# Three sums of weight blocks computed beside the convolution's projections, and the feed-forward's output gate started one chunk pair later

## The chip, the cores and the metric

The kernel runs on one core of a Trainium2 chip. A core has a matrix engine (PE, with its weight loads PEld), a vector engine (DVE), a scalar engine (ACT), GpSimd (POOL) and a queue engine (SP) that issues most transfers; 16 DMA engines move data between the chip's memory and the core. The metric is the device time of one launch in microseconds (us), lower is better. The kernel before took 958.01 us, the median of three runs (955.35 to 959.51).

## The reference, cut to what matters

One decoder block in float32, 512 tokens (S) of 1024 features (D): two mixers side by side, merged by sigmoid gates, then a SwiGLU feed-forward of 2816 hidden features. All matrix products are wanted to float32 accuracy.

```python
mod = silu(c) @ ada_w + ada_b                       # 6 vectors of 1024
sh_m, sc_m, gt_m, sh_f, sc_f, gt_f = split(mod, 6)
h = rmsnorm(x, norm_mix_g) * (1 + sc_m) + sh_m
q, k, v, g_ret, b_cv, c_cv, u_cv, g_a, g_b = split(h @ w_in, 9)
y_a = (silu(g_ret) * head_layernorm(retention(rope(q), rope(k), v))) @ ret_w_out
conv = causal_conv3(c_cv * u_cv, conv_w)
y_b = (b_cv * conv) @ conv_w_out
merged = sigmoid(g_a) * y_a + sigmoid(g_b) * y_b
x = x + gt_m * (merged @ mix_w_out)
h = rmsnorm(x, norm_ffn_g) * (1 + sc_f) + sh_f
f = (silu(h @ ffn_w_gate) * (h @ ffn_w_up)) @ ffn_w_down
x = x + gt_f * f
return rmsnorm(x, final_norm_g)
```

## The kernel before, in words

**Products.** Every float32 operand is split in a high part (ACT, a cast) and a low part (DVE, a subtraction), and a product is three matrix multiplications: high by low, low by high, high by high. A projection (`proj`) covers 256 output features: one weight load of 1 MB to a raw buffer, then for each half of 128 features a split and 24 matrix multiplications of 128 x 512. The raw buffers (tag `raw`) are three, and every large transfer uses one: a new load waits in SP's queue, in order, until the buffer it takes is given back. The split weights (tags `hi`, `lo`) have four buffers each, so that a split may run at most four halves ahead of PE.

**Stages in order of the program.** Values, keys, queries and gates of the retention, whose own steps are laid out between later projections by a counter (`after`, `tick`: each half of a projection is one tick); the convolution's projections for feature pairs p = 1 to 3, each c, u and b (in this text the convolution's loop); the loop over p = 0 to 3 with gate a, the retention's output product and 512 of the modulation's weights (`ada_load`, `mod_vecs`; the ga loop); the loop with gate b and the convolution's output product (the gb loop); the mix product in two halves of 512 columns, with the second norm between its token tiles; the feed-forward.

**Block sums.** The down product of the first 16 hidden chunks is done in two parts of eight chunks, each as a product of 2 x 2 blocks with seven multiplications in place of eight. It needs four sums of weight blocks per part. `block_sums` is a generator with eight steps, four per part: a step loads 1 MB of the down weights (two DMAs from SP) to a raw buffer, does four subtractions in place on DVE, and stores 1 MB to a scratch tensor from POOL's queue; its buffer is free when the store has landed. `next(block_steps)` does one step. Before, part 0's four steps stand at the end of the ga loop's four rounds, part 1's in the feed-forward.

**Output gates.** `gate_vec` computes gt_m or gt_f, spread over all partitions: for each of four pieces of 256 columns, at one tick a load of 1 MB (`ada_gt_m`, `ada_gt_f`), eight multiply-adds on DVE (`acc_gt_m`, `acc_gt_f`) and a split (`gh`, `gl`), and at the next tick a product with a matrix of ones on PE that spreads it (`gp_gt_m`, `gp_gt_f`). The gate gt_m is begun after the gb loop's first round; gt_f is begun after the first of part 0's four chunk pairs (q = 0).

**What sets the order.** In these stages the order on an engine is not the order of the text: the framework's scheduler places each instruction by its own account of when its inputs are ready, at compile time. On the chip each engine then runs its list in order. An instruction that waits holds everything behind it on its engine.

Of the kernel before, what the change touches and what calls it, by code (L numbers as in the profile page):

```python
# [70 lines left out]
def block_kernel(ctx, tc, x, c, positions, ada_w, ada_b, norm_mix_g, w_in, conv_w, ret_w_out,  # L71
# [18 lines left out]
    def scr(name, dt=F32, shape=None):  # L90
        return tp.tile(shape or [P, S], dt, tag="scr", bufs=12, name=name)

    def misc(name, dt=F32):
        return tp.tile([P, S], dt, tag="misc", bufs=6, name=name)

    def acc(name):
        return ps.tile([P, S], F32, tag="acc", bufs=4, name=name)
# [7 lines left out]
    def load_raw(src, k0, nk, n0, nn, name):  # L105
        t = wp.tile([P, nk, nn], F32, tag="raw", bufs=3, name=name)
        with tc.issue_after(load_raw.last.ins):
            load_raw.last = nc.sync.dma_start(
                t, src[k0 * P:(k0 + nk) * P, n0:n0 + nn].rearrange("(k p) n -> p k n", p=P))
        return t  # L110

    def split(view, shape, name, eng=None):
        hi = wp.tile(shape, F32R, tag="hi", name=name + "_h")
        act.copy(hi, view)
        lo = wp.tile(shape, F32R, tag="lo", name=name + "_l")
        (eng or vec).tensor_tensor(lo, view, hi.bitcast(F32), ALU.subtract)
        return hi, lo

    def split_act(src, name, hi=None, lo=None, eng=None):
        hi = slot(name + "_h", F32R) if hi is None else hi  # L120
        lo = slot(name + "_l", F32R) if lo is None else lo
        act.copy(hi, src)
        (eng or vec).tensor_tensor(lo, src, hi.bitcast(F32), ALU.subtract)
        return hi, lo
# [113 lines left out]
    def mod_vecs(f, j):  # L238

        pt = aux(f"mod_{f}{j}")  # L240
        a = ada_sum(ada_raw.pop((f, j)), 4 * P, f"{f}{j}")
        for i in range(4):
            mm(pt[:, i:i + 1], lhsT=a[:, i * P:(i + 1) * P], rhs=ones32[:, 0:1],
               start=True, stop=True)
        mod_cols(f, j, pt)
# [309 lines left out]
    def tick():  # L555
        due = [e for e in later if e[0] <= 1]
        later[:] = [[n - 1, fn] for n, fn in later if n > 1]
        for _, fn in due:
            fn()
# [4 lines left out]
    def conv_taps(p, i, pt, u, cv):  # L564
        vec.tensor_tensor(u, pt, u, ALU.mult)
        f = 2 * p + i
        cw = [vecs[0][:, R_CW + 8 * t + f:R_CW + 8 * t + f + 1] for t in range(3)]
        vec.tensor_scalar_mul(cv, u, cw[2])
        vec.scalar_tensor_tensor(cv[:, 1:S], u[:, 0:S - 1], cw[1], cv[:, 1:S], ALU.mult, ALU.add)
        vec.scalar_tensor_tensor(cv[:, 2:S], u[:, 0:S - 2], cw[0], cv[:, 2:S], ALU.mult, ALU.add)  # L570
# [66 lines left out]
    def fm_gemm(pt, wh, wl, Ah, Al, ts=slice(0, S)):  # L637
        for k in range(KT):
            xh, xl = (Ah[:, k, ts], Al[:, k, ts]) if Al is not None else Ah[k]
            kh, kl = (wh[k], wl[k]) if isinstance(wh, list) else (wh[:, k, :], wl[:, k, :])  # L640
            mm3(pt[:, ts], kh, kl, xh, xl, k == 0, k == KT - 1)
        return pt

    def proj(src, col, Ah, Al, name, eng=None):
        raw = load_raw(src, 0, KT, col, 2 * P, "w_" + name)
        for i in range(2):
            wh, wl = split(raw[:, :, i * P:(i + 1) * P], [P, KT, P], f"w_{name}{i}", eng)
            yield i, fm_gemm(acc(f"p_{name}{i}"), wh, wl, Ah, Al)
            tick()
# [101 lines left out]
    def block_sums():  # L751
        for part, (f0, nf) in enumerate(PARTS[:2]):
            for k in range(nf // 2):
                w = wp.tile([P, 2, D], F32, tag="raw", bufs=3, name=f"w_bl{part}{k}")
                for i in range(2):
                    r0 = (f0 + k + i * nf // 2) * P
                    with tc.issue_after(load_raw.last.ins):
                        load_raw.last = nc.sync.dma_start(w[:, i], ffn_w_down[0, r0:r0 + P, :])
                (b11, b12), (b21, b22) = ([w[:, i, j * S:(j + 1) * S] for j in range(2)]
                                          for i in range(2))  # L760
                vec.tensor_tensor(b11, b12, b11, ALU.subtract)
                vec.tensor_tensor(b12, b22, b12, ALU.subtract)
                vec.tensor_tensor(b22, b22, b11, ALU.subtract)
                vec.tensor_tensor(b21, b21, b22, ALU.subtract)
                nc.gpsimd.dma_start(blocks[part][:, k], w)
                yield

    block_steps = block_sums()
# [4 lines left out]
    for p in range(1, KT // 2):  # L773
        cc, uu = {}, {}
        for i, pt in proj(wi, COL["c"] + 2 * p * P, Hh, Hl, f"c{p}"):
            cc[i] = scr(f"c{p}{i}")
            act.copy(cc[i], pt)
        for i, pt in proj(wi, COL["u"] + 2 * p * P, Hh, Hl, f"u{p}"):
            uu[i] = scr(f"cv{2 * p + i}")
            conv_taps(p, i, pt, cc[i], uu[i])  # L780
        for i, pt in proj(wi, COL["b"] + 2 * p * P, Hh, Hl, f"b{p}"):
            vec.tensor_tensor(uu[i], pt, uu[i], ALU.mult)
            conv_in[2 * p + i] = split_act(uu[i], f"ci{2 * p + i}")


    def ret_out(p):
        raw = wp.tile([P, KT, 2 * P], F32, tag="raw", bufs=3, name=f"w_ya{p}")
        src = ret_w_out[0, :, 2 * p * P:2 * (p + 1) * P].rearrange(
            "(q h e c) n -> h e c q n", h=2, e=2, c=64)
        dst = raw.rearrange("p (q e) n -> p e q n", e=2)  # L790
        for h in range(2):
            for e in range(2):
                load_raw.last = nc.sync.dma_start(dst[64 * h:64 * h + 64, e], src[h, e])
        for i in range(2):
            wh, wl = split(raw[:, :, i * P:(i + 1) * P], [P, KT, P], f"w_ya{p}{i}")
            yield i, fm_gemm(acc(f"p_ya{p}{i}"), wh, wl, ret_in, None)
            tick()
# [5 lines left out]
    for p in range(KT // 2):  # L803
        sg = {}
        for i, pt in proj(wi, COL["ga"] + 2 * p * P, Hh, Hl, f"ga{p}"):
            sg[i] = scr(f"sga{p}{i}")
            act.activation(sg[i], pt, AF.Sigmoid)
        for i, pt in ret_out(p):
            vec.tensor_tensor(sg[i], pt, sg[i], ALU.mult)
            m_a[2 * p + i] = sg[i]  # L810
        ada_load("f", 2 * p)
        mod_vecs("f", 2 * p)
        next(block_steps)
    gate = {}

    def gate_vec(name):
# [238 lines left out]
    def block_acts(part, nf):  # L1055

        first, acts = [], {n: [] for n in ("a11", "a12", "a22", "s1", "s2", "s3", "s4")}
        tok = slice(0, HS), slice(HS, S)
        f0 = PARTS[part][0]
        for q in range(nf // 2):  # L1060
            for g in swiglu((f0 + 2 * q) * P):
                if len(first) < nf // 2:
                    k = len(first)
                    t = misc(f"a11_{part}{k}", F32R)
                    acts["a11"].append(split_act(g[:, tok[0]], "", t[:, tok[0]], t[:, tok[1]]))
                    first.append(g)
                    continue
                k = len(acts["s1"])
                a11, a21 = (first[k][:, i] for i in tok)
                a12, a22 = (g[:, i] for i in tok)  # L1070
                sums = [scr(f"s{part}{k}_{i}") for i in range(2)]
                (s1, s2), (s3, s4) = ([s[:, i] for i in tok] for s in sums)
                both = [split_act(g, f"a2_{part}{k}")]
                vec.tensor_tensor(s1, a21, a22, ALU.add)
                vec.tensor_tensor(s2, s1, a11, ALU.subtract)
                vec.tensor_tensor(s3, a11, a21, ALU.subtract)
                vec.tensor_tensor(s4, a12, s2, ALU.subtract)
                both += [split_act(s, f"s{part}{k}{i}") for i, s in enumerate(sums)]
                for i, n in enumerate(("a12", "a22", "s1", "s2", "s3", "s4")):
                    acts[n].append([z[:, tok[i % 2]] for z in both[i // 2]])  # L1080
            if part == 0 and q == 0:
                gate_vec("gt_f")
            if part == (0 if q == 3 else 1):
                next(block_steps)
        return acts
# [60 lines left out]
    for part in range(2):  # L1146
        block_down(part, block_acts(part, PARTS[part][1]))
# [78 lines left out]
```

## Time and profile before

| | before |
|---|---|
| median of three runs | 958.01 us (955.35 to 959.51) |
| the profiled execution | 957.96 us, span 956.2 us |
| granted PE clock, mean | 0.997 |
| PE busy | 940.0 us (98%) |
| DVE busy | 633.6 us (66%) |
| ACT busy | 362.1 us (38%) |
| DMA | 144.02 MB, mean 151 GB/s |

The span counts from the first to the last instruction; 1.76 us of the profiled execution lie around it. All helpers record their operations in lines 62 and 64 of the kernel, so that rows are told apart by their tiles: `w_gb_l<-w_gb,w_gb_h` is the low half of gate b's weights. A row gives its start and length in us, the engine, the operation, output and inputs, shape, count and, in brackets, the idle time before it and what ended that. PE's matrix multiplications overlap, so that the distance of their starts, not their length, is what one costs.

### The profile page before, as it was taken

The page shows a single profiled execution, that of the slowest core. Times are in us where ns is not written, and L with a number is a line of the kernel's source. Part 1 is how long each engine was busy: PE and PEld are TensorE (multiplying, and loading weights), DVE is VectorE, ACT ScalarE, POOL GpSimd, SP SyncE. Part 2 cuts the span into 40 slices and gives each one's busy share as a digit, 9 for nine tenths or more (in the row PEclk, how much of TensorE's full clock was granted, in tenths as well). Part 3 has the DMA queues.
Part 4 walks back from the last instruction along what each step waited for, and adds up shares of the span by engine and source line. Part 5 has one row for each costly group of instructions (what it writes and reads, how often), then busy time and mean ns, then how long its engine had stood idle before and what let it go on. Part 6 is the DMA issues. An engine that isn't in the chain of part 4 may idle for free.

```text
span 956.2 us, 11090 instructions
## 1 busy us (share of the span) xinstructions
PE 940.0 (98%) x4367; PEld 784.4 (82%) x4367; DVE 633.6 (66%) x981; ACT 362.1 (38%) x537; POOL 9.5 (1%) x26
## 2 busy tenths in 40 slices
PE   8999999999999999999998999999999999999997
PEld 8888888888888888888877887988888888888886
DVE  5989775899566855556367367766688536893356
ACT  7535333544444323222123234523443233532324
POOL 2000000000000000000000000000000000000000
PEclk9999999999999999999999999999999999999999
DMA  9943412332312257878556452454265752553202
GB/s 303 341 156 111 154 57 87 100 100 81 106 45 88 88 135 223 249 246 270 176 166 186 134 174 88 155 176 176 88 214 182 258 182 88 170 175 118 66 22 88
DMA packets 113619, 144.02 MB, mean 151 GB/s; under 512 B 4180, under 2 KB 93312, under 8 KB 112544
## 3 DMA queue, kind: packets, MB, share of 16 engines
q1 hardware_dynamic: 112048, 134.50, 44.3%
q0 software_dynamic: 1376, 8.57, 2.4%
q8 instruction: 34, 0.56, 0.3%
q10 hardware_dynamic: 144, 0.26, 0.1%
q14 instruction: 17, 0.14, 0.0%
HBM read 132.83 MB, written 10.49 MB: 150 GB/s over the span
## 4 chain that ended last, share of the span: by engine, by line
PE 81%; DMA 9%; DVE 7%; ACT 1%; issue 1%; SPq 1%; DVEq 0%; ACTq 0%
PE p_fu L64 12%; PE p_fg L64 12%; PE p_g L64 5%; PE p_v L64 5%; PE dn_t L64 5%; PE p_q L64 4%; PE p_k L64 4%; PE p_b L64 3%; PE p_u L64 3%; PE p_c L64 3%; PE dn_b L64 3%; DMA ada_gt_m<-in_ada_w_dram 3%; PE dn L64 3%; PE p_yb L64 2%; DMA blocks<-w_bl 2%; PE mix L64 2%
## 5 line engine op out<-in xcount | busy, mean ns | idle before, releaser
L64 PE MATMUL p_fg<-Gh,w_fg_l 128*128 128x512 f32 x160 | 62.3, 389 | 0.0
L64 PE MATMUL p_fg<-Gh,w_fg_h 128*128 128x512 f32 x160 | 62.3, 389 | 0.0
L64 PE MATMUL p_fu<-Gh,w_fu_l 128*128 128x512 f32 x160 | 62.3, 389 | 0.0
L64 PE MATMUL p_fg<-Gl,w_fg_h 128*128 128x512 f32 x160 | 62.2, 389 | 0.0
L64 PE MATMUL p_fu<-Gh,w_fu_h 128*128 128x512 f32 x160 | 62.2, 389 | 0.0
L64 PE MATMUL p_fu<-Gl,w_fu_h 128*128 128x512 f32 x160 | 62.2, 389 | 0.0
L64 DVE TENSOR_TENSOR w_fg_l<-w_fg,w_fg_h 128x1024 fp32r<-128x1024 f32 x20 | 24.4, 1222 | 33.1 <-ACT w_fg_h L64 33.1
L64 ACT CAST w_fu_h<-w_fu 128x1024 fp32r<-128x1024 f32 x20 | 21.1, 1053 | 63.7 <-PE p_fu L64 41.3
L64 ACT ACTIVATE fg<-p_fg 128x512 f32<-128x512 f32 x22 | 13.2, 598 | 76.0 <-PE p_fg L64 76.0
L64 DVE TENSOR_TENSOR w_b_l<-w_b,w_b_h 128x1024 fp32r<-128x1024 f32 x18 | 22.0, 1223 | 29.6 <-ACT w_b_h L64 29.6
L64 DVE TENSOR_TENSOR fg<-p_fu,fg 128x512 f32<-128x512 f32 x22 | 15.2, 691 | 38.6 <-PE p_fu L64 38.5
L64 PEld LDWEIGHTS p_fu<-Gl,w_fu_h 128*128 128x128 f32 x160 | 30.0, 188 | 6.2
L64 PEld LDWEIGHTS p_fg<-Gl,w_fg_h 128*128 128x128 f32 x160 | 30.0, 188 | 6.2
L64 PEld LDWEIGHTS p_fu<-Gh,w_fu_l 128*128 128x128 f32 x160 | 30.0, 188 | 6.2
L64 PEld LDWEIGHTS p_fg<-Gh,w_fg_h 128*128 128x128 f32 x160 | 30.0, 188 | 6.2
L64 PEld LDWEIGHTS p_fu<-Gh,w_fu_h 128*128 128x128 f32 x160 | 30.0, 188 | 6.2
L64 PEld LDWEIGHTS p_fg<-Gh,w_fg_l 128*128 128x128 f32 x160 | 30.0, 188 | 6.2
L64 DVE TENSOR_TENSOR sm<-st,dec 128x512 f32<-128x512 f32 (+3 forms) x32 | 15.6, 486 | 20.9 <-PE st L64 20.6
L64 DVE TENSOR_TENSOR w_bl<-w_bl 128x512 f32<-128x512 f32 x32 | 22.1, 689 | 8.0 <-DMA w_bl<-in_ffn_w_down_dram 7.4
L64 DVE TENSOR_TENSOR w_fu_l<-w_fu,w_fu_h 128x1024 fp32r<-128x1024 f32 x20 | 24.4, 1220 | 3.9 <-ACT w_fu_h L64 3.8
L64 PE MATMUL p_gb<-Hh,w_gb_l 128*128 128x512 f32 x64 | 25.2, 393 | 1.5 <-DVE w_gb_l L64 1.5
L64 ACT CAST sh<-sm 128x512 fp32r<-128x512 f32 (+3 forms) x32 | 14.7, 459 | 30.2 <-DVE sm L64 30.2
(420 smaller groups left out, 2732.5 us busy)
## 6 DMA issues: line engine op xcount, KB each, us to landing
w_fg<-in_ffn_w_gate_dram SPq DMA_DIRECT2D x11, 1024.0 KB, 5.6
w_fu<-in_ffn_w_up_dram SPq DMA_DIRECT2D x11, 1024.0 KB, 5.4
ada_m<-in_ada_w_dram SPq DMA_DIRECT2D x32, 256.0 KB, 5.8
ada_f<-in_ada_w_dram SPq DMA_DIRECT2D x32, 256.0 KB, 4.4
w_bl<-in_ffn_w_down_dram SPq DMA_DIRECT2D x16, 512.0 KB, 4.6
blocks<-w_bl POOLq DMA_DIRECT2D x8, 1024.0 KB, 6.1
w_t<-blocks SPq DMA_DIRECT2D x8, 1024.0 KB, 5.8
w_b<-in_ffn_w_down_dram SPq DMA_DIRECT2D x6, 1024.0 KB, 5.1
```

What stands on the lines that cost most here:

```text
L64: self.last = op(*args, **kw)
```

## The change

One block-sum step is put into each of the convolution's three rounds, between the c and the u projection. The ga loop keeps one step, in its first round. So the four steps of part 0 run earlier, and the ga loop's rounds 1 to 3 have none. The gate gt_f is begun after the second chunk pair (q = 1) instead of the first, so its eight ticks fall into pairs 2 and 3 instead of 1 and 2.

```diff
         for i, pt in proj(wi, COL["c"] + 2 * p * P, Hh, Hl, f"c{p}"):
             cc[i] = scr(f"c{p}{i}")
             act.copy(cc[i], pt)
+        next(block_steps)
         for i, pt in proj(wi, COL["u"] + 2 * p * P, Hh, Hl, f"u{p}"):
             uu[i] = scr(f"cv{2 * p + i}")
             conv_taps(p, i, pt, cc[i], uu[i])
...
         ada_load("f", 2 * p)
         mod_vecs("f", 2 * p)
-        next(block_steps)
+        if p == 0:
+            next(block_steps)
...
-            if part == 0 and q == 0:
+            if part == 0 and q == 1:
                 gate_vec("gt_f")
             if part == (0 if q == 3 else 1):
                 next(block_steps)
```

Three places show how the instructions move. The first is DVE in the convolution's first round, where the second of the moved sums (`w_bl_2740`) comes to stand among the retention's score products (`sm`), their splits (`sl`) and the splits of the b weights (`w_b_l`):

```order
L64 TENSOR_TENSOR sl_0_2302<-sm_0_2299,sh_0_2301 128x512
+L64 TENSOR_TENSOR w_bl_2740<-w_bl_2740 128x512
L64 TENSOR_TENSOR sm_7_2352<-st_7_2348,dec_2183 128x128
+L64 TENSOR_TENSOR w_bl_2740<-w_bl_2740 128x512
L64 TENSOR_TENSOR ci_l<-cv_722,ci_h 128x512
-L64 TENSOR_TENSOR w_b_l<-w_b_2553,w_b_h 128x1024
+L64 TENSOR_TENSOR w_b_l<-w_b_2561,w_b_h 128x1024
L64 TENSOR_TENSOR ci_l<-cv_727,ci_h 128x512
L64 TENSOR_TENSOR sl_7_2355<-sm_7_2352,sh_7_2354 128x128
L64 TENSOR_TENSOR sm_1_2365<-st_1_2361,dec_2293 128x384
+L64 TENSOR_TENSOR w_bl_2740<-w_bl_2740 128x512
L64 TENSOR_TENSOR sl_1_2368<-sm_1_2365,sh_1_2367 128x384
```

The score products `sm_7` and `sm_1` and their splits now have operations ahead of them that wait for the second sum's load. The second place is SP's queue from the ga loop's last round to the gate's first load; `w_ya` is the retention's output weight, `ada_f` the modulation's. Before:

```order
L108 DMA w_ga_3598<-in_w_in_dram 128x8x256
L793 DMA w_ya_3662<-in_ret_w_out_dram 64x4x256 x4
L64 DMA ada_f_0_3727<-in_ada_w_dram 128x2x256 x4
L64 DMA ada_f_4_3732<-in_ada_w_dram 128x2x256 x4
L758 DMA w_bl_3754<-in_ffn_w_down_dram 128x1024 x2
L108 DMA w_gb_3762<-in_w_in_dram 128x8x256
L108 DMA w_yb_3826<-in_conv_w_out_dram 128x8x256
L820 DMA gt_m_3898<-in_ada_b_dram 128x512
L820 DMA gt_m_3899<-in_ada_b_dram 128x512
L108 DMA w_gb_3902<-in_w_in_dram 128x8x256
L828 DMA ada_gt_m_3935<-in_ada_w_dram 128x8x256
```

And with the change:

```order
L108 DMA w_ga_3606<-in_w_in_dram 128x8x256
L794 DMA w_ya_3670<-in_ret_w_out_dram 64x4x256 x4
L64 DMA ada_f_0_3735<-in_ada_w_dram 128x2x256 x4
L64 DMA ada_f_4_3740<-in_ada_w_dram 128x2x256 x4
L108 DMA w_gb_3762<-in_w_in_dram 128x8x256
L108 DMA w_yb_3826<-in_conv_w_out_dram 128x8x256
L822 DMA gt_m_3898<-in_ada_b_dram 128x512
L822 DMA gt_m_3899<-in_ada_b_dram 128x512
L108 DMA w_gb_3902<-in_w_in_dram 128x8x256
L830 DMA ada_gt_m_3935<-in_ada_w_dram 128x8x256
```

The block sum's load is gone from between the modulation's and gate b's weights, and with it one user of a raw buffer; the order from there on is the same. The third place is DVE at the second norm of the first token tile, in the mix product's second half:

```order
L62 TENSOR_TENSOR n_0_r<-n2s_4404 128x1
-L64 TENSOR_SCALAR acc_gt_f_5071<-ada_gt_f_5069,cs 128x256
-L64 SCALAR_TENSOR_TENSOR acc_gt_f_5071<-ada_gt_f_5069,cs,acc_gt_f_5071 128x256 x3
L62 RECIPROCAL n_0_r<-n_0_r 128x1
-L64 SCALAR_TENSOR_TENSOR acc_gt_f_5071<-ada_gt_f_5069,cs,acc_gt_f_5071 128x256
L62 TENSOR_SCALAR xn_00_4623<-x_0_0_4386,n_0_r 128x512
L62 TENSOR_SCALAR xn_01_4625<-x_0_1_4387,n_0_r 128x512
-L64 SCALAR_TENSOR_TENSOR acc_gt_f_5071<-ada_gt_f_5069,cs,acc_gt_f_5071 128x256
L62 TENSOR_SCALAR h_00_4658<-tx_00_4648,a_f,s_f 128x128 x2
-L64 SCALAR_TENSOR_TENSOR acc_gt_f_5071<-ada_gt_f_5069,cs,acc_gt_f_5071 128x256 x2
```

The gate's sums no longer stand between the norm's statistics, its reciprocal and the scaled rows (`xn`); they come after the last `Gl` of the fourth token tile.

## The prediction

> **What bounds the kernel now.** I read first the page's busy table, then the table by stage (stage by stage the length, then busy time and count of PE, PEld, DVE, ACT and POOL, the granted clock, DMA share and GB/s), then PE's rows in order of time for every place where it sat idle.
>
> ```profile
> PE 940.0 (98%) x4367; PEld 784.4 (82%) x4367; DVE 633.6 (66%) x981; ACT 362.1 (38%) x537; POOL 9.5 (1%) x26
> ```
>
> ```profile
> 255.80:363.10 107.30, 107.30 (x491) 89.22 (x490) 73.14 (x100) 40.29 (x60) 0.00 (x0) 1.00 0.32 98
> 363.10:453.60 90.50, 90.50 (x417) 75.51 (x415) 51.60 (x74) 23.19 (x27) 2.15 (x4) 1.00 0.80 249
> 453.60:549.10 95.50, 90.91 (x394) 73.93 (x394) 49.98 (x81) 24.99 (x35) 0.00 (x0) 0.98 0.52 165
> ```
>
> The stages are the convolution's loop, the ga loop (gate a and the retention's output) and the gb loop (gate b and the convolution's output). PE sets the time. It never idles in the convolution and ga loops, though the four sums of weight blocks make DMA 80% busy in the latter. It idles in the gb loop (90.91 of 95.50), in the mix product and once after it. The rows where it does:
>
> ```profile
> 480.71 0.39 PE L64 MATMUL p_gb<-Hh,w_gb_h 128*128 128x512 f32 x1
> 482.57 0.50 PE L64 MATMUL p_gb<-Hh,w_gb_l 128*128 128x512 f32 x1 [1.47 <-DVE w_gb_l L64]
> ...
> 514.33 0.58 PE L64 MATMUL gp_gt_m<-gl_gt_m,onesr 128*128 128x256 f32 x1 [2.82 <-DVE gl_gt_m L64]
> ...
> 515.35 0.63 PE L64 MATMUL p_yb<-ci_l,w_yb_h 128*128 128x512 f32 x1
> 515.78 0.63 PE L64 MATMUL p_yb<-ci_h,w_yb_h 128*128 128x512 f32 x1
> ...
> 583.15 1.09 PE L62 MATMUL tx<-ident,xn 128*128 128x128 f32 x8 [1.92 <-DVE xn L62]
> ...
> 611.77 0.38 PE L64 MATMUL p_fg<-Gl,w_fg_4h 128*128 128x256 f32 x1 [0.58 <-DVE Gl L62]
> ```
>
> ```profile
> 527.24 0.24 PE gp_gt_m L64 x2
> 538.39 10.88 PE p_yb L64 x48
> ```
>
> The gb loop's work is eight such stretches of 10.88 and four spreads of 0.24, 88.0 us; it lasts 95.5. So 7.5 us are lost there, of them 2.82 and 1.47 in the two rows above, and some 1.3 by matmuls that after the long wait start 0.43 us apart (515.35, 515.78) where 48 normally take 10.88, 0.227 each.
>
> Why DVE is late there stands in the chain of waits:
>
> ```profile
> 445.73 8.83 DMA blocks<-w_bl
> ...
> 454.62 0.38 SPq L108
> ...
> 455.10 8.56 DMA ada_gt_m<-in_ada_w_dram
> ...
> 469.64 8.24 DMA ada_gt_m<-in_ada_w_dram
> ...
> 483.01 8.89 DMA ada_gt_m<-in_ada_w_dram
> ```
>
> ```profile
> 463.69 0.36 DVE L64 TENSOR_SCALAR acc_gt_m<-ada_gt_m,cs 128x256 f32<-128x256 f32 x1 [11.41 <-DMA ada_gt_m<-in_ada_w_dram]
> 481.30 1.22 DVE L64 TENSOR_TENSOR w_gb_l<-w_gb,w_gb_h 128x1024 fp32r<-128x1024 f32 x1
> ```
>
> Three raw buffers serve all weights. The ga loop's fourth block sum keeps one until its store lands (445.73 + 8.83 = 454.56). SP waits for that with the gb load at 454.62, and the first gate load stands behind it. The sums of the gate, and the weight splits queued behind them on DVE, then run one load after the other: 455.1, 469.6, 483.0.
>
> **The change, part by part.**
>
> *Three block sums leave the ga loop.* Per sum one 1 MB load in two DMAs, four DVE operations (692 ns in the row of the convolution part below, some 0.65 apart), one 1 MB store. The four instructions and two DMAs cost PE nothing where they leave, since PE was full there; the gain is the earlier start of the gb loop's chain. Without the store the gb load at 454.62 takes the buffer of the last retention-output weights, and the first gate load needs only the buffer of the gb weights before it. That one is free when its second split is done, and this split waits for PE to leave the last ga product:
>
> ```profile
> 441.96 0.39 PE L64 MATMUL p_ya<-ri_h,w_ya_l 128*128 128x512 f32 x1
> ```
>
> So 441.96, ACT's cast and DVE's 1.2: about 444.2 in place of 455.1. It lands near 453 (8.6 as in the chain), and its sum of eight operations at 0.5 (1.53 for three in the row at 580.65 below), with what DVE does between, ends near 457 in place of 468.5. From there each load follows the sum before it: 458 and 471 for 469.6 and 483.0, some 12 us earlier. The split that PE awaited at 482.57 is then done near 470, and the third spread's operand near 503, where PE without waits arrives at 508.6. Every wait of this loop has 5 us of cover and more, so I take nearly the whole: **-7.4**. Bounds: 0 (the chain is self-paced and stays) and 7.5.
>
> [...]
>
> *The feed-forward's gate starts one chunk pair later.* Its loads and sums stood inside the second norm, in DVE's queue:
>
> ```profile
> 573.82 6.41 DMA ada_gt_f<-in_ada_w_dram
> ```
>
> ```profile
> 578.77 0.16 DVE L62 TENSOR_TENSOR n_r<-n2s 128x1 f32<-128x1 f32 x1 [0.85 <-ACT n_j L62]
> 580.26 0.35 DVE L64 TENSOR_SCALAR acc_gt_f<-ada_gt_f,cs 128x256 f32<-128x256 f32 x1 [1.33 <-DMA ada_gt_f<-in_ada_w_dram]
> 580.65 1.53 DVE L64 SCALAR_TENSOR_TENSOR acc_gt_f<-ada_gt_f,cs,acc_gt_f 128x256 f32<-128x256 f32 x3
> 582.09 0.15 DVE L62 RECIPROCAL n_r<-n_r 128x1 f32<-128x1 f32 x1
> ...
> 609.72 0.35 DVE L64 TENSOR_SCALAR acc_gt_f<-ada_gt_f,cs 128x256 f32<-128x256 f32 x1 [1.50 <-DMA ada_gt_f<-in_ada_w_dram]
> ```
>
> The reciprocal needs only ACT's root (some 0.6 after 578.77, the norm's add, so 579.4); it ran at 582.09, and PE's transposes at 583.15 in place of about 581.1, where its matmuls before ended (583.15 less the wait). Without the four operations the norm is ready at 580.5: the wait of 1.92 goes, with its restart about 2.1. The Gl row that PE awaited at 611.77 stood behind three gate operations that began at 609.72; that wait of 0.58, 0.7 with restart, goes too. **-2.8**, bounds -2.0 and -2.9.
>
> Where do the gate's sums go? Into chunk pairs three and four, each load (5.6 to 7.6 us to landing) queued behind a split that frees its buffer.
>
> ```profile
> DMA to landing us min/median/max: 5.6/6.3/7.6
> ```
>
> ```profile
> 666.36 0.24 PE gp_gt_f L64 x2
> 666.60 10.91 PE p_fg L64 x48
> 677.51 10.88 PE p_fu L64 x48
> ```
>
> With each load at 7, sums of eight operations at 0.5 and the splits paced by PE, I get the four sums done at about 618, 633, 648 and 660. Their spreads stand in PE's queue at 652, 663, 674.3 (677.5 less 2.8, one 0.24 spread fewer ahead) and 685.4. The third is the tight one: its low half is queued on DVE behind the third pair's sums and splits and comes near 671, 3.5 us ahead of PE. Cost taken 0; with each of three loads 2 us later than I took, some 2.5. The next block sum's load moves from 646.5 to about 657; its product is not read before the second part of the feed-forward.
>
> *Three block sums enter the convolution's loop*, between the c and the u weights. PE is full there, so this can only cost. DVE is 68% busy; three sums add 12 x 0.65 = 7.8 us to 73.1 in 107.3, which fits on average. Two things are added: the DVE operations wait in order for their load, and each sum holds a raw buffer until its store lands (4.1 to 8.8 us). The first and third sum's rows fall into idle DVE time, or ahead of work with 2 us and more to spare. The second is the tight one:
>
> ```profile
> DMA to landing us min/median/max: 3.6/4.7/8.8
> ...
> L64 DVE TENSOR_TENSOR w_bl<-w_bl x32: 677/692/695, 362.7 to 760.4; 128x512 f32<-128x512 f32 x32
> ```
>
> ```profile
> 257.22 0.37 SPq L108 DMA_DIRECT2D w_u<-in_w_in_dram  x1
> ```
>
> ```profile
> 258.87 0.69 DVE L64 TENSOR_TENSOR sl<-sm,sh 128x512 fp32r<-128x512 f32 x1 [0.74 <-ACT sh L64]
> 261.72 0.29 DVE L64 TENSOR_TENSOR sm<-st,dec 128x128 f32<-128x128 f32 x1 [2.16 <-PE st L64]
> ...
> 266.66 0.56 DVE L64 TENSOR_TENSOR sl<-sm,sh 128x384 fp32r<-128x384 f32 x1 [0.63 <-ACT sh L64]
> ```
>
> ```profile
> 268.67 0.28 PE L64 MATMUL y<-sl,v_h 128*128 128x128 f32 x1
> 269.48 0.34 PE L64 MATMUL y<-sl,v_h 128*128 128x384 f32 x1
> ```
>
> Its load takes the buffer that at 257.22 went to the next u weights, behind the c load that waits for the first sum's store (done near 256). It lands at 257.65 + 4.7 = 262.4, between 261.3 and 266.4. DVE, idle from 259.5, stands at its first operation until then; behind it wait the score products and their splits (sm, sl) that PE reads at 268.67 and 269.48. After landing these need 4.1 and 5.7 us (two or three sums of 0.6, a split of 1.1, three of 0.6 and less). So PE waits only if the load lands after 263.8. Cost taken **+0.3**, bounds 0 and 2.6 (landing at 266.4), with a clock dip 3.9. The next u and b loads move from 257 and 272 to about 272 and 277; PE reads them at 308 and 320, so that is covered.
>
> **Sum.** The profiled execution took 957.96 us (span 956.2 and 1.76 around it), as good as the median of 958.01. 957.96 - 7.4 - 2.8 + 0.3 = **948.1**.
>
> **Rivals.**
>
> *The gb loop stays as it is.* DVE's order there is unchanged, and its period of load and sum, 14.5 and 13.4 us between the gate loads, is longer than the 10.9 that PE leaves. If it paced itself from the start, only the 2.8 would be won: 955.2. Against it: the second load waited for sums that began at 463.69 only because the first was issued at 455.1.
>
> *Part given back.* The second block sum's load lands late (2.6, clock dip 1.3) or the third spread comes late (2.5): 951 to 954. For it: DVE at both places waits in order for a load.
>
> *VectorE and the raw buffers become the bound in the convolution's loop.* Slower than before. Each sum then costs its full 2.6 on DVE and 2.8 of landing wait (259.5 to 262.4): 3 x 5.4 = 16.2 less 10.2 is +6, **964**. It decides when the three sums together cost PE more than 10.2, so when DVE has no idle time left before the score products. For it, ten-microsecond stretches where DVE is full:
>
> ```profile
> 290.00:300.00 10.00, 10.00 (x47) 8.04 (x46) 9.70 (x15) 5.24 (x10) 0.00 (x0) 1.00 0.33 105
> ```
>
> Against it: the order puts none of the new operations in such a stretch; it puts them where DVE in the trace is at 241, 247, 260 to 270 and 302 to 308 us, and the row at 261.72 shows it idle there for 2.16.
>
> **How the numbers follow.** Forecast 0.74, the loop that stays 0.09, part given back 0.09, slower 0.08; the strict reading of the clock rule, 949.4, is about a tenth of the forecast's share. Two kernels of this length can be told apart from about 0.5% on, 4.8 us, so faster means below 953.2. The forecast and most of the third case are faster: 0.80. Same: the second case and the rest, 0.12. Slower: 0.08. Range: the best of the bounds, 957.96 - 7.5 - 2.9 = 947.6, less 2.7 by which the runs before lie below their median, gives 945; above, the part given back and nearly the loop that stays: 955.
>
> **What would show it.** Right: PE without idle rows between 453 and 622, spreads of gt_m unwaited, no slow matmuls, the first gate load near 444, the ga loop's DMA share well below 0.80. The convolution's loop stays within 0.5 us of 107.3. Wrong: idle PE before a `y<-sl` row near 268 or before `gp_gt_f` near 674 (third case); acc_gt_m still waiting 5 us and more for loads with PE behind it (second); 110 us and more for the convolution's loop (slower).

## The result, and the profile after

The changed kernel takes 947.43 us (median of four runs, 947.26 to 948.23) and the kernel before 957.87 us beside it (955.35 to 959.51). The ratio is 0.9895, with a 95% interval of 0.9872 to 0.9917: faster by 1.05%. The prediction was 948.1 us in a range of 945 to 955. The profiled execution took 947.26 us, with a span of 945.2.

The first line of the page of after, the busy time of each engine:

```profile
PE 936.5 (99%) x4367; PEld 783.7 (83%) x4367; DVE 634.4 (67%) x981; ACT 363.2 (38%) x537; POOL 9.5 (1%) x26
```

The table by stage of after, in the columns of the prediction's table; the rows are the convolution's loop, the ga loop and the gb loop:

```profile
254.71:362.01 107.30, 107.30 (x492) 89.25 (x491) 77.75 (x108) 40.32 (x60) 1.07 (x2) 1.00 0.45 146
362.01:452.51 90.50, 90.50 (x417) 75.52 (x415) 47.35 (x68) 23.17 (x27) 0.53 (x1) 1.00 0.69 204
452.54:540.74 88.20, 88.20 (x395) 73.11 (x394) 47.83 (x75) 25.76 (x35) 0.00 (x0) 1.00 0.49 154
```

PE is busy in the whole of all three, at the full clock. The convolution's loop carries the three sums (DVE 77.75 in place of 73.14 us) and is not longer. The gb loop is shorter by 7.3 us. The places that the prediction spoke of, from the time-ordered rows of SyncE (SP), VectorE (DVE) and PE: first the loads of the gate gt_m,

```profile
443.87 0.59 SPq L830 DMA_DIRECT2D ada_gt_m<-in_ada_w_dram  x1
455.47 0.57 SPq L830 DMA_DIRECT2D ada_gt_m<-in_ada_w_dram  x1
468.95 0.55 SPq L830 DMA_DIRECT2D ada_gt_m<-in_ada_w_dram  x1
```

then VectorE at the second norm, and PE's transposes behind it,

```profile
570.41 0.16 DVE L62 TENSOR_TENSOR n_r<-n2s 128x1 f32<-128x1 f32 x1 [0.85 <-ACT n_j L62]
572.01 0.16 DVE L62 RECIPROCAL n_r<-n_r 128x1 f32<-128x1 f32 x1 [1.45 <-ACT n_r L62]
572.21 0.48 DVE L62 TENSOR_SCALAR xn<-x,n_r 128x512 f32<-128x512 f32 x1
```

```profile
572.75 1.09 PE L62 MATMUL tx<-ident,xn 128*128 128x128 f32 x8
```

The transposes have no bracket, so PE did not wait; the reciprocal comes 1.6 us after the norm's add, where it came 3.3 us after it before. With the first matrix multiplications of the stages as bounds (the mix product is counted to the start of its last one), the two profiled executions compare so (us):

| stage | before | after | difference |
|---|---|---|---|
| up to the convolution's loop | 255.78 | 254.70 | -1.08 |
| convolution's loop | 107.32 | 107.30 | -0.02 |
| ga loop | 90.55 | 90.55 | 0.00 |
| gb loop | 95.46 | 88.20 | -7.26 |
| mix product with the second norm | 48.14 | 46.11 | -2.03 |
| first chunk pair's projections | 24.90 | 24.00 | -0.90 |
| the rest | 334.04 | 334.32 | +0.28 |

Of the last two rows 0.24 is one spread of gt_f, which now stands in the rest. The two kernels are the same up to the convolution's loop, so that the 1.08 us there are not the change's; the 9.9 that are left are. In the other profiled kernels but one the convolution's loop begins at 254.73 to 255.29 us, so the profiled execution of the kernel before began it late.

### The profile page after: what moved, and what is told of

The parts are those of the page before. It is cut to its first block, busy times and chain, and to the rows that moved or that the text cites. A ratio compares the mean times of both kernels' runs of the same rounds, so it can differ in the third digit from the quotient of the medians.

```text
span 945.2 us, 11083 instructions
## 1 busy us (share of the span) xinstructions
PE 936.5 (99%) x4367; PEld 783.7 (83%) x4367; DVE 634.4 (67%) x981; ACT 363.2 (38%) x537; POOL 9.5 (1%) x26
## 3 DMA queue, kind: packets, MB, share of 16 engines
q1 hardware_dynamic: 112048, 134.50, 44.7%
## 4 chain that ended last, share of the span: by engine, by line
PE 98%; DVE 0%; ACT 0%; issue 0%; POOL 0%; ACTq 0%; POOLq 0%
PE p_fu L64 13%; PE p_fg L64 12%; PE p_ga L64 5%; PE p_g L64 5%; PE p_gb L64 5%; PE p_v L64 5%; PE p_yb L64 5%; PE dn_t L64 5%; PE p_ya L64 5%; PE p_q L64 5%; PE p_k L64 4%; PE p_b L64 3%; PE p_u L64 3%; PE p_c L64 3%; PE dn_b L64 3%; PE dn L64 3%
## 5 line engine op out<-in xcount | busy, mean ns | idle before, releaser
L64 ACT CAST w_fu_h<-w_fu 128x1024 fp32r<-128x1024 f32 x20 | 21.1, 1054 | 60.5 <-PE p_fu L64 34.2
L64 DVE SCALAR_TENSOR_TENSOR acc_f<-ada_f,cs,acc_f 128x512 f32<-128x512 f32 x28 | 21.0, 750 | 8.7 <-DMA ada_f<-in_ada_w_dram 7.8
L64 ACT CAST w_b_h<-w_b 128x1024 fp32r<-128x1024 f32 x18 | 18.9, 1051 | 18.6 <-PE p_fu L64 8.0
```

Of the source, the lines that this page charges most:

```text
L64: self.last = op(*args, **kw)
```

## The experiments

All of them are edits of the changed kernel. Times are medians, with the 95% interval of the ratio to the kernel before that ran beside them (its medians there lay between 956.3 and 958.1 us).

**One part alone: the sums.** The gate's start is put back:

```diff
-            if part == 0 and q == 1:
+            if part == 0 and q == 0:
                 gate_vec("gt_f")
```

> Only the three block sums move to the convolution's loop; the feed-forward's gate begins where it did before. Theory (the parts are independent): the gb loop takes 88.0 us instead of 95.5, the second norm keeps its two waits (about 1.9 us before the first transposes, 0.6 us before the first product with Gl), so about 950.2 us, 2.8 above the full change. Rival (the second norm's waits came from everything being late behind the gb loop): the waits go here too and the time is that of the full change, 947.4 us.

951.1 us (ratio 0.9897 to 0.9943). The gb loop takes 88.20 us, and the second norm keeps its waits, as the theory of independent parts has it. PE's rows there:

```profile
575.26 1.77 PE L62 MATMUL tx<-ident,xn 128*128 128x128 f32 x8 [2.04 <-DVE xn L62]
576.68 0.77 PE L62 MATMUL mix<-w_mix_h,mg_l 128*128 128x512 f32 x1
...
605.74 0.39 PE L64 MATMUL p_fg<-Gl,w_fg_4h 128*128 128x256 f32 x1 [0.80 <-DVE Gl L62]
```

The transposes and the multiplications behind them run slow here (1.77 us for eight, where the kernel before takes 1.09; the granted clock of the stage is 0.97), so the stage of the mix product takes 49.90 us, 1.8 more than in the kernel before, which waited 1.92 us at this place and kept its clock (1.00). That makes up the 1.7 us by which the profiled execution (951.93 us) lies above the expected 950.2; the median lies 0.9 above.

**The other part alone: the gate.** The four sums stay in the ga loop:

```diff
             act.copy(cc[i], pt)
-        next(block_steps)
...
-        if p == 0:
-            next(block_steps)
+        next(block_steps)
```

> Only the feed-forward's gate begins one chunk pair later; the four block sums stay in the ga loop. Theory: the second norm's two waits go and nothing else changes, about 955.1 us (2.8 below before), the gb loop still 95.5 us. Rival (the gate only pays where the loads before it are early): nothing is won, 957.9 us.

953.26 us (0.9926 to 0.9967), against 955.1 expected. The mix product takes 46.11 us and the first pair's projections 24.01, so the gate's part is worth 2.03 + 0.66 without the other. The gb loop takes 95.15 us, nearly the 95.46 of before. The profiled execution took 954.5 us and reached the convolution's loop 0.8 us sooner than that of the kernel before; with that, the expectation holds. That the median lies 1.2 us below the profiled execution is left open.

**Only the last of the three sums is moved.** The ga loop keeps a sum in rounds 0, 1 and 2, the fourth round has none, and the convolution's loop has one:

```diff
-        next(block_steps)
+        if p == 2:
+            next(block_steps)
...
-        if p == 0:
+        if p < 3:
             next(block_steps)
```

> One block sum in the convolution's loop (its third round), and the ga loop keeps three, in its first three rounds, with none in the fourth; the gate as in the full change. Theory (the fourth sum's hold of a raw buffer until its store lands is all that made the gate loads late): the first gate load is issued near 444 us and the gb loop takes 88.0 us, so 947.4 us, as the full change. Rival (the transfers of the sums crowd the ga loop's loads, a share for each sum): a third of the gain in the gb loop is there, its 95.5 us become 93.0, and the time is about 952.4 us.

947.63 us (0.9870 to 0.9907): the whole gain, and the gb loop at 88.20 us. The other two moves add nothing to it. What costs is a sum in the ga loop's last round.

```profile
445.35 0.59 SPq L831 DMA_DIRECT2D ada_gt_m<-in_ada_w_dram  x1
```

**The bytes without the buffer, first try.** A copy of 1 MB inside the device's memory in each of the ga loop's rounds 1 to 3, issued by GpSimd:

```diff
+        else:
+            nc.gpsimd.dma_start(spare[p], ffn_w_down[0, p * 2 * P:(p + 1) * 2 * P, :])
```

> The full change, and in the second to fourth round of the ga loop a copy of 1 MB within the device's memory that uses no buffer of the kernel: the bytes of the three sums are moved again where they were, with no raw buffer held and no work on VectorE. Theory (the buffer, not the bytes): the ga loop's DMA share rises again to about 0.8 and the time stays at 947.4 us within 0.5. Rival (the bytes): the loads of the gate come as late as before, the gb loop takes about 95.5 us and the time is about 954.9 us.

956.92 us (0.9979 to 1.0002), near the rival's number, but for another reason. The copies wait for nothing, and GpSimd's queue issued all three at the start of the program, between 5.6 and 8.3 us. The table by stretch of its first 60 us, this kernel:

```profile
0.00:20.00 20.00, 10.67 (x71) 10.28 (x72) 5.24 (x14) 10.87 (x25) 7.04 (x21) 0.91 0.88 316
20.00:60.00 40.00, 39.60 (x211) 34.25 (x211) 32.24 (x62) 19.80 (x35) 0.00 (x0) 0.96 1.06 338
```

and after:

```profile
0.00:20.00 20.00, 17.96 (x129) 17.43 (x130) 10.42 (x26) 14.65 (x33) 5.23 (x18) 1.00 0.94 304
```

PE is busy for 10.67 of the first 20 us in place of 17.96, and the convolution's loop begins at 264.06 us in place of 254.70. From there on nothing is lost (gb loop 88.20). So the run says nothing on the question; it prices 3 MB in the start-up, where the DMA share is 0.94 without them, at 9.4 us.

**The bytes without the buffer, in their place.** The same copies in SyncE's queue, where the sums' loads had stood:

```diff
+        else:
+            with tc.issue_after(load_raw.last.ins):
+                load_raw.last = nc.sync.dma_start(
+                    spare[p], ffn_w_down[0, p * 2 * P:(p + 1) * 2 * P, :])
```

> As traffic, but the three copies of 1 MB stand in SyncE's queue where the loads of the three sums stood in the kernel before, so that they run in the second to fourth round of the ga loop. Theory (the buffer, not the bytes): the ga loop's DMA share rises from 0.69 towards 0.8, the first gate load is still issued near 444 us, the gb loop takes 88.0 us and the time is 947.4 us within 0.5. Rival (the bytes): the gate's loads come late again, the gb loop takes some 95 us and the time is about 954.9 us.

947.34 us (0.9875 to 0.9908). The ga loop, and the first gate load behind it:

```profile
362.00:452.50 90.50, 90.50 (x417) 75.49 (x415) 44.98 (x64) 23.05 (x27) 0.53 (x1) 1.00 0.82 238
```

```profile
445.30 0.59 SPq L835 DMA_DIRECT2D ada_gt_m<-in_ada_w_dram  x1
```

The DMA share is 0.82, as high as before the change (0.80), the gate load comes as early as in after, and the gb loop takes 88.20 us. The bytes are not the cause.

**Six sums in the convolution's loop,** two in each round:

```diff
         next(block_steps)
+        next(block_steps)
...
-        if p == 0:
-            next(block_steps)
...
-            if part == (0 if q == 3 else 1):
+            if part == 1 and 1 <= q < 3:
                 next(block_steps)
```

> Two block sums in each of the three rounds of the convolution's loop, six in all, none in the ga loop, and the last two where they were; the gate as in the full change. Theory (the loop has room on VectorE, and only a load that lands late costs): VectorE is busy 85.6 of 107.3 us there, a second sum queued behind the first costs PE up to 1 us a round, the loop takes 107.3 to 110.3 us and the time is 947.4 to 950.4 us. Rival (VectorE and the raw buffers bound the loop from here on): each further sum costs its full 5.4 us of work and landing wait, the loop takes about 123 us and the time is about 963 us.

953.06 us (0.9935 to 0.9964), between the two: the loop takes 112.83 us, 5.5 more. Its row in the table by stretch, SyncE at the second round's loads, VectorE, and PE's wait:

```profile
255.17:368.00 112.83, 107.95 (x492) 89.09 (x491) 82.07 (x115) 40.20 (x60) 2.13 (x4) 1.00 0.59 191
```

```profile
257.48 15.55 SPq L758 DMA_DIRECT2D w_bl<-in_ffn_w_down_dram  x4
```

```profile
277.19 0.69 DVE L64 TENSOR_TENSOR w_bl<-w_bl 128x512 f32<-128x512 f32 x1 [5.36 <-DMA w_bl<-in_ffn_w_down_dram]
...
283.16 0.68 DVE L64 TENSOR_TENSOR sq_l<-sq,sq_h 128x512 fp32r<-128x512 f32 x1
```

```profile
283.90 0.50 PE L64 MATMUL var<-sq_l,blkr 128*128 128x512 f32 x1 [2.89 <-DVE sq_l L64]
```

VectorE is idle for 31 of the 113 us, so it is not full. It stands for 5.36 us at the second sum, whose load waited for a raw buffer, and the layer norm's `sq_l` behind it comes too late for PE. The same happens in the third round (1.76 us of PE's time). This is the mechanism that the prediction feared for the second sum; with one sum a round there is a free buffer, with two there is none.

**A held buffer without the sum.** At the end of the ga loop's last round a raw buffer is taken with a small load, touched by one VectorE operation of 128 x 8, and sent to memory and back in a chain of small transfers:

```diff
+        if p == 3:
+            w = wp.tile([P, 2, D], F32, tag="raw", bufs=3, name="w_hold")
+            with tc.issue_after(load_raw.last.ins):
+                load_raw.last = nc.sync.dma_start(w[:, 0, 0:8], ffn_w_down[0, 0:P, 0:8])
+            vec.tensor_tensor(w[:, 0, 0:8], w[:, 0, 0:8], w[:, 0, 0:8], ALU.add)
+            for i in range(3):
+                nc.gpsimd.dma_start(spare[i], w[:, 0, 0:8])
+                if i < 2:
+                    nc.gpsimd.dma_start(w[:, 0, 0:8], spare[i])
```

> The full change, and at the end of the ga loop's fourth round a raw buffer is taken and held, without the sum: 4 KB are loaded into it, VectorE adds 128x8 elements, and the buffer goes to the device's memory and back in five transfers of 4 KB, one after the other, at some 2 us each, so that it comes free near 455 us. Nearly no bytes and no work are added. Theory (the held buffer alone makes the gate's loads late): the gb load and the first gate load behind it are issued near 455 us, the gb loop takes 93 to 95.5 us and the time is 952 to 955 us; each us by which the buffer comes free earlier than 455 gives some of it back. Rival (the sum's work or its bytes, or the two together, made them late): the gb loop takes 88.2 us and the time is 947.4 us.

948.18 us (0.9885 to 0.9931), gb loop 88.20. The transfers were quicker than expected: the first gate load was issued at 449.23, which is still covered. Two kernels with longer chains (`range(4)` and `range(5)`, store and load each time) followed:

> As hold_only, with eight transfers of 4 KB in place of five (each took some 2 us there, and the buffer came free at 448.7 us), so that the raw buffer comes free near 454.6 us, as in the kernel before. Theory (the held buffer alone): the first gate load is issued near 455.1 us, the gb loop takes 93 to 95.5 us in place of 88.2 and the time is 952.5 to 955 us. Rival (a held buffer is covered; the sum's work on VectorE or its bytes are needed for the loss): 88.2 us, and 948 us.

> As hold_long with ten transfers, so that the buffer comes free some 4 us later, near 458.6 us. Theory: PE already waits for every further us of delay there, so the gb loop is about 4 us longer than in hold_long and the time is 956 to 959 us. Rival: as for hold_long, 948 us.

hold_long takes 949.47 us (0.9905 to 0.9958; its five runs lie between 947.6 and 953.5), hold_longer 953.63 us (0.9934 to 0.9974); neither median is what its theory or its rival gave. In both the buffer went to the first gate load, and the gb weights' load, which in the kernel before waits with it, went out early. SyncE in hold_long, and its gb loop:

```profile
443.93 0.38 SPq L108 DMA_DIRECT2D w_gb<-in_w_in_dram  x1
...
455.34 0.59 SPq L839 DMA_DIRECT2D ada_gt_m<-in_ada_w_dram  x1
```

```profile
452.60:540.80 88.20, 88.20 (x395) 73.11 (x395) 49.99 (x81) 25.16 (x35) 0.10 (x1) 1.00 0.52 167
```

In this execution that went against the theory: the first gate load is as late as in the kernel before (455.10), and nothing is lost. But it is the fastest of the five (947.59 us). The other four took 949.4 to 953.5 us and have no profile, so what the late start cost in them stays open. In hold_longer the first gate load went out at 463.80, and the gb loop lost 6.3 us. The last kernel has six transfers of 128 KB (columns `0:256`) in the form in which both loads wait for the buffer:

> As hold_only, where the held buffer is the one that the gb weights' load takes and the first gate load follows right behind it, with six transfers of 128 KB in place of five of 4 KB, so that both loads are issued near 455 us, as in the kernel before. (In hold_long and hold_longer the held buffer went to the first gate load alone, and the gb weights were loaded at 444 us; there the gb loop lost nothing with the first gate load at 455.3 us.) Theory as it stands after those runs (it takes both: the late start and the gate load behind a weights' load, whose landing then takes 7.6 to 8.9 us in place of 5.6, so that each turn of load and sum is 2 to 3 us longer): turns of 13 to 14.5 us as in hold_only and before, the fourth gate load is issued at 494 to 498 us, PE waits 2 us and more before the third spread, the gb loop takes 91 to 95.5 us and the time is 950.5 to 955 us. Rival (neither is the cause; the sum's own work or its 1 MB store decide): 88.2 us and 948 us.

948.6 us (0.9896 to 0.9947; five runs, 947.8 to 951.7). The two loads went out at 452.57 and 453.06, not near 455, and the gb loop takes 88.61 us: PE waits a little, once. That is nearer to the rival's number, though the one wait is where the theory has it.

What goes with the loss in all these profiled executions is the start of the fourth gate sum, which the third spread stands behind in VectorE's queue. The row in before and in after:

```profile
503.69 0.35 DVE L64 TENSOR_SCALAR acc_gt_m<-ada_gt_m,cs 128x256 f32<-128x256 f32 x1 [3.75 <-DMA ada_gt_m<-in_ada_w_dram]
```

```profile
488.64 0.35 DVE L64 TENSOR_SCALAR acc_gt_m<-ada_gt_m,cs 128x256 f32<-128x256 f32 x1 [1.82 <-DMA ada_gt_m<-in_ada_w_dram]
```

Taken from each kernel's first matrix multiplication of the gb loop, so that kernels can be set side by side:

| kernel | first sum starts | fourth sum starts | gb loop |
|---|---|---|---|
| sums_only | -3.2 | 35.0 | 88.20 |
| after | -3.0 | 36.1 | 88.20 |
| traffic_sp | -0.4 | 39.2 | 88.20 |
| last_only | 1.9 | 41.0 | 88.20 |
| hold_only | 4.0 | 42.4 | 88.20 |
| hold_long | 8.4 | 42.8 | 88.20 |
| hold_pair | 8.4 | 44.7 | 88.61 |
| before | 10.0 | 50.0 | 95.46 |
| gate_only | 10.8 | 51.2 | 95.15 |
| hold_longer | 19.0 | 52.6 | 94.49 |

Without waits PE reaches the third spread at 55.0. A fourth sum that starts by 43 is in time for it, one at 44.7 costs 0.4 us, and one at 50 and later 6.3 to 7.3. The fourth sum does not carry the whole of that: the first spread, which comes ahead of it, is at 34.5 in the kernel before, 37.0 in gate_only and 34.2 in hold_longer, where 32.7 is free, because PE waited for splits (`w_gb_l`) behind an earlier sum. From the first sum to the fourth it takes 40.0 us in the kernel before, 39.1 in after and 33.6 to 36.3 in the three with a long hold, so a late start can be made good where the turns are short.

The length of a turn goes with the landing of its load (8.56, 8.24 and 8.89 us for the first three of the kernel before, by the prediction's chain of waits). In all the profiles together, the 26 gate loads issued at most 1.2 us behind a weights' load landed after 7.6 to 9.2 us. The 25 with no weights' load from 3 us ahead of them to 1 us behind landed after 5.4 to 5.8, but for one at 6.9. The long landings need none of the sum's transfers: after has 8.35 and 7.71 for its second and third load, hold_only 7.62, 7.70 and 7.67. In hold_long the weights' loads went out 2 us and more ahead of the gate loads, and the turns are short. No run holds both loads back to 455 us, as in the kernel before; that the held buffer by itself makes the whole loss rests on the waits in its trace and was not shown by a run.

**PE waits of known length.** VectorE repeats the first scaling of the second norm 5, 8, 9 and 9 times for the four token tiles; run twice.

```diff
             xn2[t, h] = scr(f"xn2_{t}{h}")
+            for _ in range((5, 8, 9, 9)[t] if h == 0 else 0):
+                vec.tensor_scalar_mul(xn2[t, h], x1[t][h], r)
```

> The full change, with VectorE repeating the first scaling of the second norm 5, 8, 9 and 9 times for the four token tiles, so that PE sits idle before the transposes of the tiles for about 2.1, 2.6, 3.1 and 3.5 us. Theory (the clock is judged in windows that run on their own, so the length of a wait does not decide alone): half-speed matmuls follow some of the four waits, and not strictly the longer ones. Rival (a threshold in the wait's length near 2.8 us, as the profile before suggested): they follow the last two waits and not the first two. Time about 947.4 + 11.3 + 1.3 for each slow stretch, so 960 to 964 us.

> The same kernel as idle_a once more. Theory (windows that run on their own): the same waits are followed by half-speed matmuls at other places, or by more or fewer of them, than in idle_a. Rival (a threshold in the wait's length): the same places and the same number of slow matmuls as in idle_a.

963.15 and 964.85 us, one run each; the second lies just above the expected 960 to 964. PE's rows in the first execution:

```profile
575.53 1.10 PE L62 MATMUL tx<-ident,xn 128*128 128x128 f32 x8 [2.50 <-DVE xn L62]
576.38 0.48 PE L62 MATMUL mix<-w_mix_h,mg_l 128*128 128x512 f32 x1
...
585.40 1.06 PE L62 MATMUL tx<-ident,xn 128*128 128x128 f32 x8 [3.31 <-DVE xn L62]
...
595.87 1.94 PE L62 MATMUL tx<-ident,xn 128*128 128x128 f32 x8 [3.93 <-DVE xn L62]
```

and in the second:

```profile
575.98 1.97 PE L62 MATMUL tx<-ident,xn 128*128 128x128 f32 x8 [2.50 <-DVE xn L62]
577.60 0.78 PE L62 MATMUL mix<-w_mix_h,mg_l 128*128 128x512 f32 x1
...
587.12 1.07 PE L62 MATMUL tx<-ident,xn 128*128 128x128 f32 x8 [3.15 <-DVE xn L62]
...
597.58 1.94 PE L62 MATMUL tx<-ident,xn 128*128 128x128 f32 x8 [3.92 <-DVE xn L62]
```

The same wait of 2.50 us is followed by slow transposes (1.97 us) in one execution and by quick ones (1.10) in the other; waits of 3.31 and 3.15 are not, waits of 3.9 are in both. PE did not wait for the fourth tile's transposes, so the runs have three such waits and not four. The length of a wait alone does not decide.

## Why the prediction was right, and where it was not

- **The gb loop, -7.4.** Measured -7.26. PE's idle rows between 453 and 622 are gone, and the slow multiplications with them. The "clock rule" behind the 949.4 among the chances, by which they would stay without the wait, is shown by no run; in after the granted clock of the whole loop is 1.00. The rows that the prediction priced, 2.82, 1.47 and 1.3, are 5.6 of its 7.5 us. The four spreads show where the rest lies: counted from the loop's start, they come 1.8, 2.6, 5.7 and 7.3 us later in before than in after, so the restart after the first wait and a delay at the second spread cost some more. The first gate load was put at 444.2, the next at 458 and 471; they came at 443.87, 455.47 and 468.95, on a clock that runs 1.08 us ahead of before's. The cover was put at 5 us and more; the fourth sum's start had 6.7 to 8.6 us to spare (36.1, where 42.8 was free and 44.7 was not), and the third low half was ready at 499.23, 8.3 us ahead of PE.
- **Its reason holds here, but not as a rule.** "The second load waited for sums that began at 463.69 only because the first was issued at 455.1" is right for these two kernels: the fourth sum comes 13.9 us earlier (50.0 to 36.1), of which 13.0 are the earlier start of the first and 0.9 shorter turns. A late start by itself need not cost that: hold_long issued the first gate load just as late and lost nothing in its profiled execution, where its turns were 11.5, 11.2 and 11.7 us in place of 14.2, 14.0 and 11.8. hold_longer, whose first gate load went out 8.5 us later still, lost 6.3 in spite of short turns. The part that takes the fourth sum of the ga loop for the culprit stands: moving it alone gave all of the gain (last_only), and the bytes of the sums in the same place gave no loss (traffic_sp).
- **The gate, -2.8.** Measured -2.03 at the transposes (2.1 predicted) and, without the moved spread, -0.66 at Gl (0.7 predicted). The part is worth the same with the sums left in place (gate_only). That nothing was lost at the transposes is partly luck: the prediction had the reciprocal 0.6 us behind the norm's add, it came 1.6 us behind it, and the first scaled rows were ready at 572.69, 0.06 us before PE took them.
- **The second sum, +0.3.** Measured 0. Its load was put at 262.4 and its first operation ran at 260.76, 1.08 us of it by the earlier clock; VectorE stood there for 2.28 us and the score products behind it were still in time:

```profile
260.76 0.69 DVE L64 TENSOR_TENSOR w_bl<-w_bl 128x512 f32<-128x512 f32 x1 [2.28 <-DMA w_bl<-in_ffn_w_down_dram]
...
266.42 0.56 DVE L64 TENSOR_TENSOR sl<-sm,sh 128x384 fp32r<-128x384 f32 x1
```

```profile
268.40 0.34 PE L64 MATMUL y<-sl,v_h 128*128 128x384 f32 x1
```

  The split ends at 266.98 and PE reads it at 268.40, 1.4 us later. So the place is tight, and six_sums showed the same mechanism at work two rows further on.
- **The third spread of gt_f, 0.** Its low half was put at 671, 3.5 us ahead of PE. It was ready at 659.4, 6.4 us ahead. (Both times of the prediction leave out the 7.4 us by which the gb loop ends earlier, and 677.5 less 2.8 and 0.24 is 674.5, not 674.3.)

```profile
658.99 0.42 DVE L64 TENSOR_TENSOR gl_gt_f<-acc_gt_f,gh_gt_f 128x256 fp32r<-128x256 f32 x1
```

```profile
665.78 0.28 PE L64 MATMUL gp_gt_f<-gl_gt_f,onesr 128*128 128x256 f32 x1
```

- **The sum.** 957.96 less 9.9 by the prediction; 9.9 measured in the stages that the change touches, and 1.08 us of a shorter start-up on top in this execution, less 0.3 that lies around the span. The terms miss by 0.1, 0.1 and 0.3 us, which cancel in part; that the profiled execution lies 0.8 us below 948.1 is the start-up, for which the forecast has no term.
- **The rivals.** "The gb loop stays" and "part given back" did not come. "VectorE and the raw buffers bound the loop" did not come either; six sums in place of three bring it on, at 5.5 us rather than 16.2, because only two of the waits reach PE.

## What to carry to other kernels

Ask of a shared buffer who takes it next, and what stands in the queue behind that load: here one sum of the three was all that counted. A chain of loads that each wait for the sum before ends at its start plus its turns, and both must be read; the number to watch is when its last member lands against when the consumer arrives. Work put beside a full engine was free here as long as each of its loads found a free buffer: one sum per round fits where two do not.

## What was not expected of the hardware

**The clock after a wait.** PE's multiplications ran slow (0.43 us from start to start in place of 0.23, or 1.77 to 1.97 us for eight transposes in place of 1.06 to 1.10) after waits of 1.85 us (gate_only), 2.04 (sums_only), 2.50 (idle_b), 2.82 (before) and 3.9 (both idle runs), and not after 2.44 (gate_only), 2.50 (idle_a), 2.89 (six_sums), 3.15 (idle_b) and 3.31 (idle_a). The shortest that did and a longer one that did not, in one execution of gate_only:

```profile
482.62 0.59 PE L64 MATMUL p_gb<-Hh,w_gb_l 128*128 128x512 f32 x1 [1.85 <-DVE w_gb_l L64]
483.00 0.63 PE L64 MATMUL p_gb<-Hl,w_gb_h 128*128 128x512 f32 x1
...
514.71 0.39 PE L64 MATMUL gp_gt_m<-gl_gt_m,onesr 128*128 128x256 f32 x1 [2.44 <-DVE gl_gt_m L64]
514.93 0.28 PE L64 MATMUL gp_gt_m<-gh_gt_m,onesr 128*128 128x256 f32 x1
```

The multiplications of 483.00 and after start 0.43 us apart, those after 514.93 0.23. In the kernel before the granted clock falls to 0.50 at 514.12 us, in the wait of 2.82, is back at 1.00 at 517.53, 3.41 us later, and falls next at 954.43, which is 128 times 3.41 us after that. The 3.41 us ahead of the first fall and the slow stretch itself, in the columns of the prediction's table:

```profile
510.71:514.12 3.41, 0.79 (x4) 0.33 (x2) 2.72 (x6) 2.02 (x4) 0.00 (x0) 1.00 0.75 247
514.12:517.53 3.41, 3.20 (x9) 2.63 (x10) 3.36 (x6) 3.41 (x6) 0.00 (x0) 0.50 0.26 41
```

The same about gate_only's wait of 1.85 us,

```profile
479.47:482.88 3.41, 1.56 (x7) 1.02 (x6) 3.30 (x7) 0.00 (x0) 0.00 (x0) 1.00 0.00 0
482.88:486.30 3.42, 3.42 (x9) 2.65 (x9) 3.38 (x6) 1.57 (x2) 0.00 (x0) 0.50 0.74 246
```

then two stretches of this length that share idle_a's wait of 3.31 us:

```profile
580.57:583.98 3.41, 1.53 (x7) 0.94 (x5) 3.18 (x7) 0.15 (x1) 0.00 (x0) 1.00 0.00 0
583.98:587.40 3.42, 2.00 (x13) 1.86 (x14) 3.04 (x8) 0.41 (x2) 0.00 (x0) 1.00 0.00 0
```

PE idled for 2.62 us of the stretch ahead of the fall in the kernel before (3.41 less 0.79) and for 1.85 us in gate_only (3.41 less 1.56). The wait of 3.31 us left 1.88 and 1.42 us of idle PE in its two stretches, and the clock stayed at 1.00. With 1.85 us before a fall and 1.88 without one, and ends of PE's multiplications that the profile models, these rows give no border; what makes the clock fall after one wait and not after another was not shown. A slow stretch cost 1.4 us at the first transposes: the stage of the mix product takes 58.82 us in idle_b, with two slow stretches and 0.17 us less of waiting, and 57.56 in idle_a with one.

**The spread of the runs.** The kernel before lay between 954.9 and 960.3 us in 13 runs, the changed kernel between 947.3 and 948.2 over four, last_only and traffic_sp within 0.6. hold_long, whose profile shows no loss, lay between 947.6 and 953.5. How the transfers land (5.4 to 9.2 us for the gate loads above) and whether the clock falls after a wait may be the causes; that was not shown run by run, since only one execution of each is profiled.
